# Moving a context prefix's load and normalization into the loop over the latent tokens

## The chip, the core and the metric

The kernel runs on one core of a Trainium2 chip. Five engines work side by side, each in its own fixed order: TensorE (PE, with its weight loads shown as PEld), VectorE (DVE), ScalarE (ACT), GpSimd (POOL) and SyncE (SP), whose queue issues the transfers here. They wait for each other through semaphores. Matrix products end in PSUM, eight banks of 512 columns; everything else lies in the on-chip memory SBUF. The metric is device microseconds of one execution; the times given are medians of several. Beside that time stands the span of a profiled execution, from its first to its last recorded instruction.

## What is computed

One layer of a hybrid diffusion backbone: 512 latent tokens x, 256 context tokens ctx, width 1024, all float32. The part that matters here is the beginning. Two modulation vectors come from the condition vectors, both token sets are normalized and modulated with them, and one wide projection is applied to both.

```python
mod   = silu(c) @ w_ada + b_ada            # for x
mod_c = silu(c_ctx) @ w_ada + b_ada        # for ctx
h  = rms_norm(x,   g_norm1) * (1.0 + sc1)  + sh1
hc = rms_norm(ctx, g_norm1) * (1.0 + csc1) + csh1
aq, ak, av, dq, dk, dv, dz, da, db, ga, gd = split_cols(h @ w_in)
caq, cak, cav, cdq, cdk, cdv, cdz, cda, cdb, cga, cgd = split_cols(hc @ w_in)
```

Here `da` and `db` give the decay and the write strength of a gated delta rule ("the gates"), `dk` its keys, which pass a short convolution and a silu. Windowed attention, the delta rule over chunks in both directions, the merge of the branches and the MLP follow; they are the other nine tenths of the time.

## The kernel before

Tokens lie along the columns and the 1024 features along eight groups of 128 partitions, so x is eight tiles of 128x512 and ctx eight of 128x256. For accuracy every float32 product is made as three: each operand is split into a high and a low part, and `mm3` (L308 to L315) adds high times high, high times low and low times high. A weight tile is 128 output columns with all eight feature groups; `wload` makes its high part on ACT (L259) and its low part on DVE (L262).

The start runs as follows. `rms` (L278 to L290) takes the mean square of x: ACT squares (L281), DVE adds (L284), PE sums over partitions with a matrix of ones (L286), ACT makes rstd with Ln and Exp (L148). Then a loop runs over the eight feature groups, `kt` from 0 to 7. In each turn:

- `modulate` (L317 to L321) makes h of this group for x: DVE scales (L318), ACT adds the shift and rounds to the high part (L319), DVE makes the low part (L320). ACT also keeps the unrounded h (L333) in a list `tx`.
- `ada` and `columns` make the modulation of the group two turns ahead: a 1 MB tile of w_ada is loaded (L206), multiplied on PE (L210), copied by ACT (L234), turned into columns on PE (L239) and finished on DVE (L242, L243).
- The early weight tiles, four tiles of `dk`, are loaded in turns 0 and 1, and each turn multiplies its h with all four of them, in four banks that stay open over the loop.

In turn 5 (`CTXAT` is 7, `AHEAD` is 2) the SP queue takes the weights of the gates, `wab`, and the context, two transfers, behind the last tile of w_ada.

After the loop `ab_strips` (L299 to L305) makes the gates of x: sixteen float32 products with 32 output rows each (L302), read from `tx`. A dependency that makes no wait, only an order for the scheduler, holds each group of four behind the h at position 3 of the list. Then come the statistics of the context (`rms` again), its modulation in eight steps (L318 to L320 with 256 columns, and L358 for the unrounded copy), and the context's strips. Next the four early weight tiles are multiplied with the context (96 matmuls of 256 columns), with the convolutions of `dk` on ACT and DVE (L611 to L613) among them. Then follow the gates' arithmetic (L665 to L677, exponentials and logarithms on ACT), four silus, sums of squares (L629), and the first tile of the next weights (`wh`, `wl`).

The order of the instructions on each engine is not exactly that of the program. A scheduler fixes it at compile time: it lets an engine take the earliest instruction of the program that its estimate of times says is ready. The waits are added by it as well, from the memory that instructions read and write.

Buffers come from a ring, `Arena`, of 167 units of 256 columns. `alloc` takes the next free units behind the last ones taken, and `free` releases them at once in the program's order; whoever gets the same units later waits on the chip for the earlier users. So which buffer falls on which units decides some of the waits. Banks of PSUM come from a second ring of eight.

Of the kernel before, what the change touches and what calls it, by code (L numbers as in the profile page):

```python
# [11 lines left out]
AF = mybir.ActivationFunctionType  # L12
# [10 lines left out]
LEAD = 0  # L23
ATT = 32
NHALF = 3
CTXAT = 7
WARM = 3, 6
NONES = 16
AHEAD = 2
# [9 lines left out]
KT = D // P  # L39
SEQ = 512  # L40
CTX = 256
# [58 lines left out]
def tile_layer(ctx: ExitStack, tc: tile.TileContext, I: dict, out: bass.AP, dbg=None):  # L100
    nc = tc.nc
    V, A, G, PE = nc.vector, nc.scalar, nc.gpsimd, nc.tensor
# [19 lines left out]
    alloc, bank = mem.get, lambda n=1: banks.get(n * 512)  # L122
# [14 lines left out]
    nosync = mybir.DependencyInfo(mybir.DependencyClass.NoSync, mybir.DependencyReason.DATA)  # L137
    actg = {"set": None, "head": None, "ops": []}

    def act(out_, in_, func, **kw):  # L140

        sets = TABLES.get(func)
        if sets and actg["set"] not in sets:
            head = A.preload_act_table_set(sets[0])
            for o in actg["ops"]:
                tc.add_manual_dep(head.ins, o.name, nosync, reason="table sets")
            actg.update(set=sets[0], head=head.ins, ops=[head.ins])
        r = A.activation(out_, in_, func, **kw)  # L148
        if sets:
            tc.add_manual_dep(r.ins, actg["head"].name, nosync, reason="table sets")  # L150
            actg["ops"].append(r.ins)
        return r
# [48 lines left out]
    def ada(kt):  # L201


        rp_ = banks.get(512, True)
        wb = alloc(2048)
        nc.sync.dma_start(out=wb.ap, in_=I["wada1"][kt])  # L206
        for half in range(2):
            for g in range(4):
                k = half * 4 + g
                PE.matmul(rp_[32 * g:32 * g + 32, :256], scond[:, k], wb[:, k * 256:(k + 1) * 256],  # L210
                          start=(half == 0), stop=(half == 1))
        wb.free()
        return rp_

    def warm(bank_, n):

        for _ in range(n):
            PE.matmul(bank_[:, 384:512], ones, ones, start=True, stop=True)

    xs_, cs_ = alloc(8 * SEQ), alloc(8 * CTX)  # L220
# [3 lines left out]
    modA = const.tile([P, KT, 2], F32, name="modA")  # L224
    modS = const.tile([P, KT, 2], F32, name="modS")
# [3 lines left out]
    def columns(kt, rp_):  # L229

        if kt == 0:
            warm(rp_, WARM[0])
        rb_ = alloc(256)
        row_[kt] = A.activation(rb_.ap, rp_[:, :256], AF.Copy)  # L234
        rp_.free()
        mp_ = banks.get(512, True)
        mp = mp_[:, 0:4].rearrange("p (h n) -> p h n", h=2)
        for half in range(2):
            PE.matmul(mp[:, half, :], rb_[:, half * P:(half + 1) * P], prm[:, 184:186], start=True, stop=True)  # L239
        rb_.free()  # L240

        V.tensor_scalar(modA[:, kt, :], mp[:, 0, :], bada1[:, kt:kt + 1], g1[:, kt:kt + 1], op0=ALU.add, op1=ALU.mult)  # L242
        V.tensor_scalar(modS[:, kt, :], mp[:, 1, :], bada[:, kt:kt + 1], None, op0=ALU.add)  # L243
        if kt == 0:
            warm(mp_, WARM[1])
        mp_.free()

    def wfetch(src, n=KT):
        raw = sb.tile([P, KT, P], F32, tag="wr", bufs=NWR, name=nm("wr"))[:, :n]
        nc.sync.dma_start(out=raw, in_=src)  # L250
        return raw

    def wload(src, n=KT, bufs=None, raw=None):
        raw = wfetch(src, n) if raw is None else raw
        if bufs:
            hi, lo = (b.ap.rearrange("p (k c) -> p k c", k=KT) for b in bufs)
        else:
            hi, lo = (sb.tile([P, KT, P], F32, tag=t, bufs=NWS, name=nm(t))[:, :n] for t in ("wh", "wl"))
        h = A.activation(r32(hi), raw, AF.Copy)  # L259
        if not early:  # L260
            tc.add_manual_dep(h.ins, row_[0].ins.name, nosync, reason="behind the first row")
        V.tensor_tensor(r32(lo), raw, hi, op=ALU.subtract)  # L262
        return r32(hi), r32(lo)

    early, EARLY = [], {T_DK: 0, T_DK + 1: 0, T_DK + 2: 0, T_DK + 3: 1}

    def load_early(raw=None):
        bb = ebufs[2 * len(early):][:2]
        early.append((wload(I["win"][list(EARLY)[len(early)]], bufs=bb, raw=raw), bank()))

    xt = [xs_[:, k * SEQ:(k + 1) * SEQ] for k in range(KT)]
    ct_ = [cs_[:, k * CTX:(k + 1) * CTX] for k in range(KT)]
    rstd = alloc(768)
    rx, rc = rstd[:, :512], rstd[:, 512:768]

    def rms(src, nt, n, r):

        ss = bank()  # L278
        for i in range(nt):
            b = alloc(1024)  # L280
            A.activation(b.ap, src[:, i * 1024:(i + 1) * 1024], AF.Square)  # L281
            w = 512
            while w >= n:
                V.tensor_tensor(b[:, :w], b[:, :w], b[:, w:2 * w], op=ALU.add)  # L284
                w //= 2
            PE.matmul(ss[:, :n], ones, b[:, :n], start=(i == 0), stop=(i == nt - 1))  # L286
            b.free()
        act(r, ss[:, :n], AF.Ln, bias=epsc, scale=1.0 / D)
        ss.free()
        act(r, r, AF.Exp, scale=-0.5)  # L290
# [6 lines left out]
    tx, tc_ = [], []  # L297

    def ab_strips(ab, hs, s):  # L299

        for g in range(4):
            m = PE.matmul(ab[32 * g:32 * g + 32], wab[:, 4 * s + g], hs[g][0].ap, start=(s == 0), stop=(s == 1))  # L302
            tc.add_manual_dep(m.ins, hs[3][1].ins.name, nosync, reason="strips together")
        for _ in range(4):
            hs.pop(0)[0].free()  # L305


    def mm3(acc, w, xs, start=True, stop=True, ks=None):  # L308
        ks = list(range(len(xs))) if ks is None else ks
        n = len(ks)  # L310
        for i, k in enumerate(ks):
            xhi, xlo = xs[i]
            PE.matmul(acc, w[0][:, k, :], xhi, start=(start and i == 0), stop=False)  # L313
            PE.matmul(acc, w[0][:, k, :], xlo, start=False, stop=False)  # L314
            PE.matmul(acc, w[1][:, k, :], xhi, start=False, stop=(stop and i == n - 1))  # L315

    def modulate(t, src, r, sc, sh, hi, lo, eng=V):  # L317
        V.scalar_tensor_tensor(t, src, sc, r, op0=ALU.mult, op1=ALU.mult)  # L318
        A.activation(r32(hi), t, AF.Identity, bias=sh)  # L319
        eng.scalar_tensor_tensor(r32(lo), t, sh, hi, op0=ALU.add, op1=ALU.subtract)  # L320
        return r32(hi), r32(lo)  # L321

    H, HCb = alloc(8 * 1024, True), alloc(8 * 512, True)
    hx, hc = [], []
    columns(1, ada(1))
    raw1 = wfetch(I["win"][T_DK + 1])
    for kt in range(KT):
        t = alloc(512)
        o = kt * 1024
        hx.append(modulate(t.ap, xt[kt], rx, modA[:, kt, 0:1], modS[:, kt, 0:1],  # L330
                           H[:, o:o + 512], H[:, o + 512:o + 1024]))
        h = alloc(512)
        tx.append((h, A.activation(h.ap, t.ap, AF.Identity, bias=modS[:, kt, 0:1])))  # L333
        t.free()
        if kt == 0:
            load_early(raw0)
            load_early(raw1)
        if kt + AHEAD < KT:
            columns(kt + AHEAD, ada(kt + AHEAD))
        if kt + AHEAD == CTXAT:  # L340
            nc.sync.dma_start(out=wab_.ap, in_=I["wab"])
            for k4 in range(KT // 4):
                nc.sync.dma_start(out=cs_[:, k4 * 1024:(k4 + 1) * 1024], in_=I["ctxT"][k4])
        if len(early) < len(EARLY):
            load_early()
        for (w, acc), k0 in zip(early, EARLY.values()):
            for k in range(kt + 1) if kt == k0 else (kt,):
                mm3(acc.ap, w, [hx[k]], start=(k == 0), stop=(k == KT - 1), ks=[k])
    abx = bank()
    for s in range(2):  # L350
        ab_strips(abx.ap, tx, s)
    rms(cs_, 2, CTX, rc)
    for kt in range(KT):
        t = alloc(256)
        o = kt * 512
        hc.append(modulate(t.ap, ct_[kt], rc, modA[:, kt, 1:2], modS[:, kt, 1:2],
                           HCb[:, o:o + 256], HCb[:, o + 256:o + 512]))
        tc_.append((t, A.activation(t.ap, t.ap, AF.Identity, bias=modS[:, kt, 1:2])))  # L358
    abc = bank()
    for s in range(2):  # L360
        ab_strips(abc[:, :CTX], tc_, s)
# [299 lines left out]
    t, t2 = alloc(TOK), alloc(TOK)  # L661
# [601 lines left out]
    for g in range(2):  # L1263
        cs_ = slice(g * 1024, g * 1024 + 1024)
        V.tensor_tensor(nv(on[:, cs_]), nv(ot_[:, cs_]), bc(osf[:, g * 16:g * 16 + 16], HD), op=ALU.mult)

    for qq in range(2):
# [3 lines left out]
        for a in range(2):  # L1271
            n = 2 * qq + a
            t = alloc(512)
# [259 lines left out]
```

## Time and profile before

| | us |
|---|---|
| runs shown | 942.98, 939.68, 942.67 |
| median | 942.67 |
| the profiled execution's own time | 939.99 |
| its span | 937.9 |

On the profile's page PE is busy 96% of the span, DVE 63%, ACT 48%. Its section on the chain that ended last follows the work back from the last instruction and says how much of the span each engine holds; that, and not the busy share, says what the end waits for. The timeline lists instructions in order of time, with the number merged into a row after "x", and in brackets the idle time of the engine before them and what ended it. The windows view gives, for a stretch of time, each engine's busy time, the clock that the throttle granted to PE (1.00 is full) and what the DMA engines moved. The transfers at the start, from their list up to 60 us: eight tiles of w_ada of 1024 KB with a median of 10.6 us from issue to landing, nine weight tiles of 512 KB with 8.1 us, two context transfers of 512 KB with 7.2 us, one of 128 KB for `wab` with 4.8 us.

### The profile page before, as it was taken

To read this page: it belongs to the slowest core of one execution; us is meant where nothing else is said; L and a number is where in the kernel's file an instruction comes from. 1 tells how busy PE (TensorE), PEld (TensorE's weight loads), DVE (VectorE), ACT (ScalarE), POOL (GpSimd) and SP (SyncE) were. 2 spreads that over 40 slices of the span, in tenths; PEclk is the share of its full clock that TensorE was granted. 3 is DMA by queue.
4 is the path that set the end of the run, shared out by engine and by line. 5 is a ranking of instruction groups with operands and counts; after the bars stand their busy time and mean duration, and the time that the engine had idled before them with its cause. 6 is when DMAs were issued, how large, how long until landed. Compare 5 with 4: busy or idle time off the path is not lost.

```text
span 937.9 us, 18101 instructions
## 1 busy us (share of the span) xinstructions
PE 900.3 (96%) x7706; PEld 724.5 (77%) x7706; DVE 595.2 (63%) x1017; ACT 451.6 (48%) x832; POOL 12.1 (1%) x26
## 2 busy tenths in 40 slices
PE   7979889999999999989999999999999999999998
PEld 4658567877777677778888888988888888888886
DVE  4485799997777899258865886982455235434411
ACT  5467845247667977575645424661243125213400
POOL 0000000000000001000000000000000000000000
PEclk9989999999999999999999999999999999999999
DMA  9631021210000132324523485481344124222111
GB/s 360 267 115 51 24 70 45 68 46 24 23 1 23 45 96 88 114 93 149 169 81 134 148 272 154 140 290 42 109 151 144 46 68 152 96 68 90 45 42 48
DMA packets 28448, 98.32 MB, mean 105 GB/s; under 512 B 3536, under 2 KB 4176, under 8 KB 27344
## 3 DMA queue, kind: packets, MB, share of 16 engines
q1 hardware_dynamic: 28368, 97.18, 31.5%
q8 instruction: 60, 0.98, 0.4%
q14 instruction: 20, 0.16, 0.1%
HBM read 95.07 MB, written 2.10 MB: 104 GB/s over the span
## 4 chain that ended last, share of the span: by engine, by line
PE 76%; DVE 12%; ACT 7%; DMA 3%; issue 2%; SPq 0%; DVEq 0%; ACTq 0%
PE banks L313 16%; PE banks L314 16%; PE banks L315 16%; PE banks L989 10%; PE banks L1034 2%; PE banks L1101 2%; DMA wa<-in_wada 2%; PE banks L564 1%; PE banks L1132 1%; PE banks L1113 1%; DVE wl L262 1%; ACT m L148 1%; PE banks L570 1%; DVE m L819 1%; DVE m L818 1%
## 5 line engine op out<-in xcount | busy, mean ns | idle before, releaser
L313 PE MATMUL banks<-m,m 128*128 128x512 f32 (+1 forms) x600 | 224.2, 379 | 5.1 <-ACT m L319 4.6
L314 PE MATMUL banks<-m,m 128*128 128x512 f32 (+1 forms) x600 | 225.2, 378 | 0.0
L315 PE MATMUL banks<-m,m 128*128 128x512 f32 (+1 forms) x600 | 225.2, 378 | 0.0
L259 ACT ACTIVATE m<-wr 128x1024 fp32r<-128x1024 f32 x68 | 71.9, 1059 | 157.9 <-PE banks L314 79.9
L313 PEld LDWEIGHTS banks<-m,m 128*128 128x128 f32 x600 | 112.8, 190 | 27.6 <-ACT m L319 6.6
L314 PEld LDWEIGHTS banks<-m,m 128*128 128x128 f32 x600 | 113.2, 190 | 22.4 <-issue 1.2
L315 PEld LDWEIGHTS banks<-m,m 128*128 128x128 f32 x600 | 113.1, 189 | 21.8 <-issue 1.6
L262 DVE TENSOR_TENSOR m<-wr,m 128x1024 fp32r<-128x1024 f32 x68 | 83.2, 1224 | 69.7 <-PE banks L314 34.2
L989 PE MATMUL banks<-m,wh 128*128 128x512 f32 x320 | 104.0, 399 | 0.0
L313 PE MATMUL banks<-m,wh 128*128 128x512 f32 (+1 forms) x280 | 102.8, 368 | 0.3 <-ACT wh L259 0.2
L315 PE MATMUL banks<-m,wl 128*128 128x512 f32 (+1 forms) x280 | 100.4, 361 | 1.5 <-DVE wl L262 1.4
L314 PE MATMUL banks<-m,wh 128*128 128x512 f32 (+1 forms) x280 | 101.6, 363 | 0.0
L1417 DVE SCALAR_TENSOR_TENSOR m<-banks,modT,m 128x512 f32<-128x512 f32 x32 | 24.0, 750 | 101.0 <-PE banks L315 101.0
L262 DVE TENSOR_TENSOR wl<-wr,wh 128x1024 fp32r<-128x1024 f32 (+1 forms) x58 | 62.3, 1073 | 25.8 <-ACT wh L259 25.6
L259 ACT ACTIVATE wh<-wr 128x1024 fp32r<-128x1024 f32 (+1 forms) x58 | 54.5, 940 | 30.0 <-PE banks L314 16.2
L989 PEld LDWEIGHTS banks<-m,wh 128*128 128x128 f32 x320 | 59.1, 188 | 12.2
L989 PE MATMUL banks<-m,wl 128*128 128x512 f32 x160 | 64.9, 406 | 0.0
L315 PEld LDWEIGHTS banks<-m,wl 128*128 128x128 f32 x280 | 53.3, 191 | 9.7 <-DVE wl L262 2.3
L313 PEld LDWEIGHTS banks<-m,wh 128*128 128x128 f32 x280 | 53.4, 191 | 8.8 <-ACT wh L259 0.7
L314 PEld LDWEIGHTS banks<-m,wh 128*128 128x128 f32 x280 | 53.5, 191 | 7.0 <-issue 0.4
L184 ACT ACTIVATE m<-m 128x512 fp32r<-128x512 f32 (+1 forms) x56 | 35.2, 631 | 48.2 <-DVE m L1400 20.8
L185 DVE TENSOR_TENSOR m<-m,m 128x512 fp32r<-128x512 f32 (+1 forms) x56 | 38.3, 689 | 18.8 <-ACT m L184 18.3
(236 smaller groups left out, 1290.0 us busy)
## 6 DMA issues: line engine op xcount, KB each, us to landing
wr<-in_wm SPq DMA_DIRECT2D x64, 512.0 KB, 3.5
wr<-in_win SPq DMA_DIRECT2D x38, 512.0 KB, 3.6
wa<-in_wada SPq DMA_DIRECT2D x32, 512.0 KB, 4.2
m<-in_wada SPq DMA_DIRECT2D x8, 1024.0 KB, 10.6
m<-in_xT SPq DMA_DIRECT2D x8, 512.0 KB, 5.2
wr<-in_wbr SPq DMA_DIRECT2D x16, 256.0 KB, 2.7
wr<-in_wout SPq DMA_DIRECT2D x8, 512.0 KB, 4.4
out<-m SPq DMA_DIRECT2D x8, 256.0 KB, 2.0
```

Source lines behind the costliest of these rows:

```text
L148: r = A.activation(out_, in_, func, **kw)
L184: A.activation(r32(hi), src, AF.Copy)
L185: (eng or V).tensor_tensor(r32(lo), src, hi, op=ALU.subtract)
L259: h = A.activation(r32(hi), raw, AF.Copy)
L262: V.tensor_tensor(r32(lo), raw, hi, op=ALU.subtract)
L313: PE.matmul(acc, w[0][:, k, :], xhi, start=(start and i == 0), stop=False)
L314: PE.matmul(acc, w[0][:, k, :], xlo, start=False, stop=False)
L315: PE.matmul(acc, w[1][:, k, :], xhi, start=False, stop=(stop and i == n - 1))
L989: PE.matmul(acc.ap, w[x][:, k, :], hx[k][y], start=(k == p == 0), stop=(k == KT - 1 and p == 2))
L1034: PE.matmul(pa.ap, w[x][:, j, :], r32(Q[y][:, :, j, :]), start=(j == p == 0), stop=(j == 3 and p == 2))
L1101: PE.matmul(z[r, x * 256 + q * HD:x * 256 + (q + 1) * HD], src[q][r, col(c):col(c) + CH], S[r, q * HD:(q + 1) * HD], start=True, stop=True)
L1417: V.scalar_tensor_tensor(xn_[ct], acc.ap, modT[:, 3, ct:ct + 1], xn_[ct], op0=ALU.mult, op1=ALU.add)
```

## The change

`CTXAT` goes from 7 to 3: the transfers of `wab` and of the context are put into turn 1 of the loop, and the load of the fourth early weight tile, in the same turn, is placed ahead of them. The statistics of the context are made at the end of turn 3 and its modulation at the ends of turns 4 to 7, two groups each. The order dependency of the strips goes to the last entry of the list: for the first four strips that is the eighth h, for the last four of the remaining list the same one. The computation is the same.

```diff
-CTXAT = 7
+CTXAT = 3
...
-            tc.add_manual_dep(m.ins, hs[3][1].ins.name, nosync, reason="strips together")
+            tc.add_manual_dep(m.ins, hs[-1][1].ins.name, nosync, reason="strips together")
...
+    def context(kt):
+
+        t = alloc(256)
+        o = kt * 512
+        hc.append(modulate(t.ap, ct_[kt], rc, modA[:, kt, 1:2], modS[:, kt, 1:2],
+                           HCb[:, o:o + 256], HCb[:, o + 256:o + 512]))
+        tc_.append((t, A.activation(t.ap, t.ap, AF.Identity, bias=modS[:, kt, 1:2])))
+
     columns(1, ada(1))
...
             columns(kt + AHEAD, ada(kt + AHEAD))
+        if len(early) < len(EARLY):
+            load_early()
         if kt + AHEAD == CTXAT:
             nc.sync.dma_start(out=wab_.ap, in_=I["wab"])
             for k4 in range(KT // 4):
                 nc.sync.dma_start(out=cs_[:, k4 * 1024:(k4 + 1) * 1024], in_=I["ctxT"][k4])
-        if len(early) < len(EARLY):
-            load_early()
         for (w, acc), k0 in zip(early, EARLY.values()):
             for k in range(kt + 1) if kt == k0 else (kt,):
                 mm3(acc.ap, w, [hx[k]], start=(k == 0), stop=(k == KT - 1), ks=[k])
+        if kt == 3:
+            rms(cs_, 2, CTX, rc)
+        if kt > 3:
+            context(2 * kt - 8)
+            context(2 * kt - 7)
     abx = bank()
     for s in range(2):
         ab_strips(abx.ap, tx, s)
-    rms(cs_, 2, CTX, rc)
-    for kt in range(KT):
-        t = alloc(256)
-        o = kt * 512
-        hc.append(modulate(t.ap, ct_[kt], rc, modA[:, kt, 1:2], modS[:, kt, 1:2],
-                           HCb[:, o:o + 256], HCb[:, o + 256:o + 512]))
-        tc_.append((t, A.activation(t.ap, t.ap, AF.Identity, bias=modS[:, kt, 1:2])))
     abc = bank()
```

## The prediction

> **What bounds the kernel now.** I read the page first: the busy times, then the chain that ended last.
>
> ```profile
> span 937.9 us, 18101 instructions
> PE 76%; DVE 12%; ACT 7%; DMA 3%; issue 2%; SPq 0%; DVEq 0%; ACTq 0%
> ```
>
> PE carries three quarters of the chain, so a change pays where PE stands still or runs slowly. The change touches only the first tenth of the span. So I cut the start into stretches: the loop over x (in two parts), the pause behind it, the context products (the 96 matmuls of 256 columns on the four early tiles), and the two stretches after. Columns: start and end, length, then busy time and count of PE, PEld, DVE, ACT and POOL, PEclk, DMA share, GB/s.
>
> ```profile
> 17.50:35.00 17.50, 14.73 (x98) 8.98 (x98) 9.81 (x17) 8.79 (x14) 0.00 (x0) 1.00 0.81 324
> 35.00:55.90 20.90, 20.90 (x143) 14.58 (x141) 9.29 (x20) 8.76 (x15) 0.73 (x1) 1.00 0.75 265
> 55.90:64.40 8.50, 3.41 (x22) 1.01 (x21) 8.47 (x16) 6.36 (x11) 0.00 (x0) 0.86 0.06 22
> 64.40:79.30 14.90, 14.90 (x111) 13.81 (x112) 12.27 (x27) 9.41 (x23) 0.73 (x1) 0.85 0.23 80
> 79.30:93.20 13.90, 13.40 (x113) 11.82 (x112) 5.80 (x14) 13.37 (x18) 0.00 (x0) 0.88 0.01 1
> 93.20:104.40 11.20, 9.07 (x68) 4.47 (x67) 4.93 (x8) 8.49 (x15) 0.00 (x0) 0.85 0.01 1
> ```
>
> From 35.0 to 55.9 PE is never idle, while DVE and ACT each use under half. From 55.9 to 64.4 it is the reverse: DVE is full and PE works 3.41 of 8.50 us. The timeline shows what PE does there; the bracket is idle time before the instruction and what ended it.
>
> ```profile
> 55.93 1.92 PE L302 MATMUL banks<-m,m 128*32 128x512 f32 x16
> 57.01 2.00 ACT L281 ACTIVATE m<-m 128x1024 f32<-128x1024 f32 x2 [0.29 <-PE banks L302]
> 59.93 0.67 PE L286 MATMUL banks<-m,ones 128*128 128x256 f32 x2 [2.08 <-DVE m L284]
> 61.53 0.79 PE L286 MATMUL banks<-m,ones 128*128 128x256 f32 x2 [0.93 <-DVE m L284]
> 64.40 1.22 PE L313 MATMUL banks<-m,m 128*128 128x256 f32 x4 [2.08 <-ACT m L319]
> 74.87 0.28 PE L313 MATMUL banks<-m,m 128*128 128x256 f32 x1
> 77.27 0.28 PE L313 MATMUL banks<-m,m 128*128 128x256 f32 x1
> 79.43 0.40 PE L313 MATMUL banks<-m,wh 128*128 128x512 f32 x1
> ```
>
> The context statistics begin only after the gate strips (L302): the square on ACT is released by them. The data were not late; the ring of buffers explains it. Walking its allocations in program order, the square's buffer falls on units that held an h of the loop, which the strips read. Then squares, adds on DVE among the convolutions, the sum on PE, the rstd and the first modulation run one after another: PE idles 2.08 + 0.93 + 2.08 = 5.09 us.
>
> The granted clock falls as well:
>
> ```profile
> 20.00:25.00 5.00, 3.75 (x27) 1.83 (x27) 2.86 (x5) 2.02 (x4) 0.00 (x0) 1.00 1.02 418
> 25.00:30.00 5.00, 3.75 (x26) 2.42 (x29) 2.86 (x5) 2.61 (x4) 0.00 (x0) 1.00 0.72 300
> 60.00:65.00 5.00, 1.99 (x7) 1.10 (x8) 4.97 (x11) 3.15 (x7) 0.00 (x0) 0.70 0.00 0
> 65.00:70.00 5.00, 5.00 (x32) 4.52 (x31) 4.97 (x13) 4.54 (x12) 0.00 (x0) 0.62 0.01 3
> ```
>
> It is 0.70 and 0.62 around the pause. At full clock a context product takes (77.27 - 74.87) / 20 = 0.12 us, the 20 matmuls between those starts being counted in the trace.
>
> **The change, part by part.**
>
> *The transfers.* The gate weights (128 KB) and two context transfers (512 KB each), 1.18 MB, move on SP's queue from behind the eighth modulation tile to behind the fourth early weight tile, ahead of four modulation tiles of 1 MB.
>
> ```profile
> 10.64 0.44 SPq L250 DMA_DIRECT2D wr<-in_win  x1
> 13.87 0.33 SPq L206 DMA_DIRECT2D m<-in_wada  x1
> 35.34 1.07 PE L210 MATMUL banks<-m,m 128*32 128x256 f32 x16
> 38.83 0.42 PE L210 MATMUL banks<-m,m 128*32 128x256 f32 x4
> ```
>
> At 13.87 SP had been waiting for a free buffer, so three more issues fit in front. At 418 GB/s the added bytes take 2.8 us. The queue is full until about 28.6 (0.72 of the slice 25 to 30), by when the sixth modulation tile has landed; it now lands near 31.4, and PE reads it at 38.83. The fifth lands one tile (2.5 us) earlier, near 28.9, and is read at 35.34. Slack is over 6 us on both: cost nothing. If the cover were gone, the 2.8 us would show. The two later tiles wait for buffers and are issued when the queue has drained. The context lands near 26, well before the fourth turn.
>
> *Statistics and modulation.* Nothing is added to the work; it moves forward. Its rows, all in 55.9 to 79.4 before:
>
> ```profile
> L358 ACT ACTIVATE m<-m,modS 128x256 f32<-128x256 f32 x8 | 3.5, 499 | 0.6 <-DVE m L320 0.6
> L319 ACT ACTIVATE m<-m,modS 128x256 fp32r<-128x256 f32 x8 | 3.5, 498 | 0.6 <-DVE m L318 0.6
> L318 DVE SCALAR_TENSOR_TENSOR m<-m,modA,m 128x256 f32<-128x256 f32 x8 | 3.4, 467 | 0.0
> L320 DVE SCALAR_TENSOR_TENSOR m<-m,modS,m 128x256 fp32r<-128x256 f32 x8 | 3.4, 467 | 0.0
> L281 ACT ACTIVATE m<-m 128x1024 f32<-128x1024 f32 x2 | 2.0, 1048 | 0.3 <-PE banks L302 0.3
> L284 DVE TENSOR_TENSOR m<-m 128x512 f32<-128x512 f32 x2 | 1.4, 688 | 0.0
> L284 DVE TENSOR_TENSOR m<-m 128x256 f32<-128x256 f32 x2 | 0.8, 415 | 0.0
> L148 ACT ACTIVATE m<-banks,epsc 128x256 f32<-128x256 f32 x1 | 0.5, 473 | 1.3 <-PE banks L286 1.3
> L148 ACT ACTIVATE m<-m 128x256 f32<-128x256 f32 x1 | 0.4, 416 | 0.0
> ```
>
> DVE: 3.4 + 3.4 + 1.4 + 0.8 = 9.0 us. ACT: 3.5 + 3.5 + 2.0 + 0.5 + 0.4 = 9.9 us. In the PE-bound part of the loop DVE would then hold 9.29 + 9.0 = 18.3 of 20.9 us and ACT 8.76 + 9.9 = 18.7. Both fit, barely, and the statistics can begin before 35, where both have gaps too. By the same walk along the ring their buffers now fall on units of the third modulation tile, read long before, so the wait on the strips is gone. What can go wrong is order: each of the last turns has a short chain, PE's modulation product, ACT's copy, PE's sum, DVE's columns, and a context operation of 0.4 us ahead of a link delays it, and with it whatever PE has queued behind. PE's four sum matmuls (L286) also enter the full loop: 0.67 + 0.79 us by their rows, less the overlap of their ends, 1.2 us. For disturbed order I bound below by 0 (PE has earlier turns' matmuls to run meanwhile) and above by 4.5 us (in each of the last four turns a link on ACT waits for a pair of context operations, 2 x 3.5 / 8 = 0.9 us, and once for a square, 1.0); I take 1.0, near the lower end, because half of both engines is empty there.
>
> *The strips held together.* The first four strips now wait for the eighth h instead of the fourth. Queued behind them on PE are the context strips and products. Before, all sixteen already ran in one piece at 55.93, after the last product of x, whose turn needs that turn's values as well: 0 us either way. The context strips, before in two pieces, become one.
>
> *Sum, first step: the start of the next weight tile* (79.43, the first product with wh). After: the loop's end 55.9, + 1.2 sums, + 1.0 order, + 1.9 strips of x, + 1.3 context strips (half as many columns, bounded by the 1.9), + 96 x 0.12 = 11.5 products = 72.8. Gain 6.6 us: 5.1 of idle, the rest mostly the clock, which has no pause left to fall in.
>
> The convolutions (DVE) and their banks don't become late: without 9.0 us of context work DVE has 8.47 + 12.27 - 9.0 = 11.7 us left for the 17 us from 55.9 to 72.8.
>
> *Second step: what is late next.* From 78.41 ACT runs the gates, table loads and silus without a pause, and PE waits for what follows.
>
> ```profile
> 78.41 0.85 ACT L148 ACTIVATE m<-m 32x768 f32<-32x768 f32 x1 [0.18 <-DVE m L667]
> 85.63 3.04 ACT L148 ACTIVATE m<-m 128x768 f32<-128x768 f32 x4
> ```
>
> ACT is busy 13.37 of 13.90 us from 79.3 to 93.2. PE idles 0.50 and 2.13 us in the last two stretches, and at clocks of 0.88 and 0.85 loses up to 0.12 x 13.9 + 0.15 x 11.2 = 3.3 us. The gates need only the strips and adds on DVE, so they can run beside the products: from some 66, 12 us earlier, against 6.6 for PE. Silus need the last product, near 73, and then run without the 6 us of gates ahead. So ACT gains more than PE and PE's waits shrink. Bounds: 0 (the gates keep their place behind) to 2.6 + 3.3 = 5.9 us. I take 2.9, about half: of the idle time 2, of the clock 0.9, since the small matmuls that precede its dip remain.
>
> Total 6.6 + 2.9 = 9.5 us. From there the kernel is the same on every engine and should shift as a whole.
>
> The sum is against the profiled execution, 939.99 us (span 937.9 and 2.1 around it): 930.5. That is 2.7 below the median shown, 942.67. I forecast medians: 942.7 - 9.5 = **933.2**.
>
> **The rivals.**
>
> *A, given back.* The pause closes but the loop is disturbed by 4.5 us, not 1.0, and the ACT stretch gives nothing: 6.6 - 3.5 = 3.1 us, 939.6. For it: 18.7 of 20.9 us on ACT leaves little room. Against: the gaps before 35.
>
> *B, not moved.* ACT takes the statistics late after all, behind the strips, because their order or a buffer holds them: about 0, 942.7. Against: the ring.
>
> *C, slower: the turn's chain becomes the bound.* If ACT's and DVE's context work (9.9 + 9.0 us) ran ahead of the links rather than beside them, the loop would grow by up to 18.9 us; it turns slower beyond 9.5. At three quarters, 14.2, it gives 942.7 + 4.7 = 947.4. Against: the two engines work at the same time, and PE has a turn of products in stock.
>
> *D, clock.* The pause is spread as many small waits over turns 4 to 7, and the clock falls there: at half clock the stretch 38.83 to 55.93 would lose up to 17.1 us, 942.7 - 9.5 + 17.1 = 950.3. Against: from 20 to 30 PE was idle a quarter of the time in small waits, and the clock stayed at 1.00. [...]
>
> **How the numbers follow.** Forecast 0.67; A 0.17; B 0.06; C 0.07; D 0.03. The forecast's terms run from 6.6 - 3.5 + 0 to 7.6 + 5.9, that is 3.1 to 13.5 us: 929.2 to 939.6. The runs shown lie 3.3 us apart, so I widen to **928 to 940**; B, C and D are left out. 0.5%, about what a measurement of this kernel can tell from no change, is 4.7 us: faster below 938.0. Of the forecast's chance 0.03 lies above that, where few of its terms come true; of A's, 0.06 lies below. Faster 0.64 + 0.06 of A = 0.70; same 0.03 + 0.11 + 0.06 + 0.01 of C = 0.21; slower 0.09.
>
> **What would show it.** Right: squares (L281, second pair) before 40 us; context modulation (L318, 256 columns) between 36 and 54; PE without idle from 35 to about 73; a granted clock of 1.00 from 55 to 72; the first product with wh near 73; the first silu near 74, not 85.63. Wrong: an x product or modulation product in turns 4 to 7 that waits for ACT or DVE by more than 1 us in sum; strips that start after 59; a gain at the wh product that is gone by 130 us, which would mean that another engine, DVE first, bounds what follows.

## The result and the profile after

The changed kernel takes 934.46 us (median of 7 runs, 928.64 to 935.11), the kernel before 942.49 in the same measurement: a ratio of 0.991, 95% interval 0.9884 to 0.9937. Measured once more, on another chip (e9 below), it was 933.89 against 939.09, 0.9935 (0.9911 to 0.9958). So 5 to 8 us were gained where 9.5 had been forecast. The profiled execution took 934.46 us, against 939.99 before, 5.5 less.

The page of the changed kernel: its span, and the chain that ended last.

```profile
span 932.4 us, 18104 instructions
PE 71%; DVE 12%; ACT 9%; DMA 5%; issue 3%; SPq 0%; DVEq 0%; ACTq 0%
```

The windows view of the changed kernel over the same stretches as before (columns as there).

```profile
17.50:35.00 17.50, 15.00 (x88) 8.50 (x88) 7.34 (x15) 7.04 (x11) 0.00 (x0) 0.80 0.87 342
35.00:55.90 20.90, 19.65 (x136) 13.12 (x135) 15.45 (x35) 15.30 (x29) 0.73 (x1) 1.00 0.62 222
55.90:64.40 8.50, 8.50 (x53) 5.09 (x54) 6.35 (x11) 6.00 (x12) 0.00 (x0) 1.00 0.32 101
64.40:79.30 14.90, 14.90 (x121) 14.11 (x113) 11.82 (x22) 6.84 (x14) 0.73 (x1) 1.00 0.22 75
79.30:93.20 13.90, 13.10 (x103) 10.61 (x102) 4.82 (x12) 12.69 (x19) 0.00 (x0) 0.88 0.00 0
93.20:104.40 11.20, 9.07 (x96) 4.92 (x98) 8.23 (x12) 9.29 (x18) 0.00 (x0) 0.85 0.01 1
```

The pause is gone: from 55.9 to 64.4 PE is busy all of 8.50 us (3.41 before), and the clock stays at 1.00 to 79.3. Three other things are new. The clock is 0.80 in the first stretch, where it was 1.00. PE has 1.25 us of idle time in the loop, where it had none. And the last two stretches are as slow as before: ACT at 12.69 of 13.90, clocks of 0.88 and 0.85.

The timeline of the changed kernel, PE and ACT, at the places that the prediction named:

```profile
36.53 2.00 ACT L281 ACTIVATE m<-m 128x1024 f32<-128x1024 f32 x2
41.02 1.07 PE L210 MATMUL banks<-m,m 128*32 128x256 f32 x16
58.16 1.04 PE L302 MATMUL banks<-m,m 128*32 128x512 f32 x2
62.09 2.78 PE L302 MATMUL banks<-m,m 128*32 128x512 f32 x30
64.80 0.39 PE L313 MATMUL banks<-m,m 128*128 128x256 f32 x1
76.05 0.40 PE L313 MATMUL banks<-m,wh 128*128 128x512 f32 x1
```

The squares start at 36.53 with no wait for the strips. The modulation product of group 4, at 35.34 before, comes at 41.02. The loop ends near 62, not 55.9; behind it the strips, all but one of x and of the context together, take 2.8 us in one piece and the products 11.2 us. The first product with wh comes at 76.05 instead of 79.43: **3.4 us gained, where 6.6 had been forecast.** The gain stays between 2.5 and 3.4 us up to 200 us, is 4.4 us at 305 us and 5.5 us at the end of the span. What adds the last microsecond, near 550 us, was not looked into.

The next view explains a part. These are windows of the kernel before (first fence) and of the changed kernel (second), laid on the places where the granted clock is low.

```profile
62.00:68.80 6.80, 4.71 (x21) 4.40 (x21) 6.77 (x17) 5.85 (x15) 0.00 (x0) 0.50 0.01 2
89.30:92.70 3.40, 3.40 (x14) 3.01 (x14) 1.66 (x5) 3.06 (x6) 0.00 (x0) 0.50 0.00 0
215.60:219.00 3.40, 3.40 (x51) 2.42 (x50) 2.46 (x5) 2.26 (x4) 0.00 (x0) 0.51 0.36 123
```

```profile
21.80:25.20 3.40, 3.28 (x20) 1.59 (x20) 1.11 (x2) 0.68 (x2) 0.00 (x0) 0.53 1.00 393
28.60:32.00 3.40, 3.09 (x13) 1.90 (x17) 1.30 (x2) 0.88 (x2) 0.00 (x0) 0.54 0.84 349
86.70:90.10 3.40, 3.40 (x16) 3.11 (x16) 1.76 (x6) 3.37 (x6) 0.00 (x0) 0.53 0.00 0
```

Taken in slices of 0.2 us, the clock in these two profiles is 1.00 or 0.50, apart from the slices in which it changes: ten falls to 0.50, one of 6.8 us (62 to 68.8 of the kernel before), nine of 3.4. The changed kernel lost the long fall in the pause, and the one at 216 us, but this profile of it has two falls in the loop that the profile of before doesn't have. By the products of groups 2 and 3 (L210, at 23.88 and 31.35 against 23.81 and 29.46, after a start that was 0.4 earlier) they cost 2.3 us up to there.

### The profile page after: what moved, and what is told of

Its sections match the earlier page's. It is cut to its first block, busy times and chain, and to the rows that moved or that the text cites. A ratio compares the mean times of both kernels' runs of the same rounds, so it can differ in the third digit from the quotient of the medians.

```text
span 932.4 us, 18104 instructions
## 1 busy us (share of the span) xinstructions
PE 900.4 (97%) x7706; PEld 723.8 (78%) x7706; DVE 595.8 (64%) x1017; ACT 451.4 (48%) x832; POOL 12.1 (1%) x26
## 4 chain that ended last, share of the span: by engine, by line
PE 71%; DVE 12%; ACT 9%; DMA 5%; issue 3%; SPq 0%; DVEq 0%; ACTq 0%
PE banks L313 15%; PE banks L314 15%; PE banks L315 15%; PE banks L996 8%; DMA wr<-in_wm 2%; PE banks L1041 2%; DMA wa<-in_wada 2%; ACT m L148 2%; PE banks L1108 2%; DVE wl L262 1%; PE banks L1139 1%; PE banks L571 1%; PE banks L1120 1%; DVE m L185 1%; DVE m L826 1%
## 5 line engine op out<-in xcount | busy, mean ns | idle before, releaser
L185 DVE TENSOR_TENSOR m<-m,m 128x512 fp32r<-128x512 f32 (+1 forms) x56 | 38.3, 689 | 18.8 <-ACT m L184 18.3
```

The lines of the kernel that those rows point to most:

```text
L185: (eng or V).tensor_tensor(r32(lo), src, hi, op=ALU.subtract)
```

## The experiments

All times are medians, each beside runs of the kernel before on the same chip; ratios are against those and, as they stand on record, need not be the quotient of the two medians. "Mean clock" is the mean over a kernel's runs of the clock granted over its span.

**e1, the transfers alone.** The kernel before, with `CTXAT` 3 and the early tile's load ahead of them:

```diff
-CTXAT = 7
+CTXAT = 3
+        if len(early) < len(EARLY):
+            load_early()
         if kt + AHEAD == CTXAT:
...
-        if len(early) < len(EARLY):
-            load_early()
```

> Only the transfers move (behind the fourth early weight tile); statistics, modulation and strips stay as before. Theory: placing the context ahead of four modulation tiles makes the scheduler put PE's modulation product of group 4 behind the stored x products, so turn 4 begins some 5 us late, while the statistics still wait for the strips: first product with wh at 80 to 83 us, time 943 to 946. Rival, the transfers cost nothing and the loop lost its time to the added work alone: modulation product of group 4 near 35, first product with wh at 79.4, time as before, 942.5.

942.1 us, ratio 1.0016 (0.9999 to 1.0032). The timeline of e1:

```profile
41.54 1.07 PE L210 MATMUL banks<-m,m 128*32 128x256 f32 x16
43.20 1.04 PE L302 MATMUL banks<-m,m 128*32 128x512 f32 x2
44.71 1.05 PE L302 MATMUL banks<-m,m 128*32 128x512 f32 x4
```

The mechanism was right: group 4's modulation product moves to 41.54 although only transfers were moved in the program, and single strips scatter into the loop. A strip is listed as two instructions, so the sixteen rows of L302 for x are eight products of the program; one alone takes 1.04 us, all eight together 1.92. The first product with wh comes at 84.92, but in the slowest of the twelve runs (945.65 us), whose mean clock is 0.986 (0.9896 over the twelve). What the moved transfers cost is not settled: 1.3 us by the medians, anything from 0 to 3 us by the interval. That the scheduler believed the modulation tile to be late is argued only; that the transfers' place moves the product is shown, here and in e2.

**e2, the transfers two turns later.** The changed kernel with

```diff
-CTXAT = 3
+CTXAT = 5
```

> The changed kernel with the transfers two turns later, behind the sixth modulation tile (CTXAT 5 in place of 3). Theory: the modulation product of group 4 comes back to 35 to 36 us from 41, the loop over x ends 2 to 4 us earlier than at 62, and the kernel gains 1.5 to 3 us on the changed one: 931.5 to 933 by the median. Rival, PE's work in the loop is only reordered and its sum bounds it: loop end and time as the changed kernel, 934.5.

933.39 us, ratio 0.9929 (0.9905 to 0.9953): not to be told from the changed kernel's 0.991 and 0.9935. The product is back in its place and PE's loop still ends at 60.6, with 18 of the 96 context products already done; 2.3 of the 62 us in the changed kernel were the clock. So the rival holds: the loop's work was only in another order. But the profiled execution of e2 (930.31 us, the fastest of its runs) had a clock of 1.00 throughout, and shows the new order without that disturbance. Its timeline and windows:

```profile
35.43 1.07 PE L210 MATMUL banks<-m,m 128*32 128x256 f32 x16
72.80 0.40 PE L313 MATMUL banks<-m,wh 128*128 128x512 f32 x1
```

```profile
20.00:25.00 5.00, 3.75 (x27) 1.84 (x27) 2.86 (x5) 2.04 (x3) 0.00 (x0) 1.00 1.02 415
25.00:30.00 5.00, 3.75 (x24) 2.41 (x28) 2.86 (x5) 2.67 (x4) 0.00 (x0) 1.00 1.02 414
```

The first product with wh is at 72.80, 6.6 us before the old place.

**e3, the strips' order as before.** The changed kernel with

```diff
-            tc.add_manual_dep(m.ins, hs[-1][1].ins.name, nosync, reason="strips together")
+            tc.add_manual_dep(m.ins, hs[3][1].ins.name, nosync, reason="strips together")
```

> The changed kernel with the strips' order as before (behind the h at position 3). Theory: the scheduler scatters single strips among the x products and each lone strip holds the whole array for about 1 us where four together take 0.4: with some five pieces 2 to 3 us more, 936 to 938. Rival, the strips only fill time in which PE waits in turns 4 and 5: same as the changed kernel, 934.5.

934.49 us, ratio 0.9931 (0.991 to 0.9952). Some strips do scatter (from 36.90 on), and it costs nothing that can be measured: the rival. The theory also counted four strips together at 0.4 us, which no run shows: here a row of eight instructions, so four strips, takes 1.06 us (at 64.41), as long as one strip alone (1.05, at 36.90). The forecast of 0 us for this edit holds.

**e4, the gates first.** The changed kernel with the block that makes the gates (from `nega` to the end of `t2.free()`, L662 to L686 of the changed kernel) moved ahead of the line `kT = [...]`, so ahead of the context products:

```diff
+    nega = const.tile([32, 1], F32, name="nega")
+    act(nega, alog[0:32], AF.Exp)
...
     kT = [alloc(TOK, True) for _ in range(4)]
     for q, (w, acc) in enumerate(early):
...
-    nega = const.tile([32, 1], F32, name="nega")
-    act(nega, alog[0:32], AF.Exp)
```

> The changed kernel with the gates' arithmetic ahead of the context products and convolutions in the program. Theory: the gates came late because their adds on DVE stand behind the convolutions; moved ahead, ACT's gate chain begins before 70 instead of 75.9, the first silu comes at 77 to 79 instead of 83.1, and 2 to 4 us are gained: 930.5 to 932.5. Rival, DVE is full there and the convolutions become late in turn, so that products wait for their banks: 934 to 936.

936.17 us, ratio 0.9948 (0.993 to 0.9966), at a mean clock of 0.991 (0.993 for e3, on the same chip). The chain of the gates does move: the table load ahead of the silus is at 75.80, 81.84 in the changed kernel. But PE waits for a late convolution, as the rival said:

```profile
69.85 0.35 PE L313 MATMUL banks<-m,m 128*128 128x256 f32 x1 [1.86 <-DVE m L620]
```

Behind this wait the clock falls (0.62 from 71.4 to 74.8), and PE takes sums of squares before the next weight tile, whose first product is at 84.41, 76.05 in the changed kernel. In this form, no gain.

**e5, buffers of their own.** The kernel before, with two buffers for the squares:

```diff
+    own = [alloc(1024), alloc(1024)]
...
-            b = alloc(1024)
+            b = own[i] if own else alloc(1024)
...
-    rms(cs_, 2, CTX, rc)
+    rms(cs_, 2, CTX, rc, own)
```

> The kernel before with two buffers of its own for the squares of the context, so that they no longer fall on the ring's units that the strips read; nothing else moves. Theory: the squares and adds run in ACT's and DVE's free time before 56, PE's pause of 5.1 us of idle shrinks to the last links (rstd, first modulation, about 3 us), and the time falls by 2 to 4 us. Rival, the squares wait for something else (the data, the order): pause and time as before.

941.54 us, ratio 1.0014 (0.9991 to 1.0037). Squares and adds do run before 56 now, so the ring did hold them. But in PE's order the sums stand behind the strips, and the wait remains. Its timeline:

```profile
57.20 1.92 PE L303 MATMUL banks<-m,m 128*32 128x512 f32 x16
59.06 1.13 PE L286 MATMUL banks<-m,ones 128*128 128x256 f32 x4
63.74 0.58 PE L314 MATMUL banks<-m,m 128*128 128x256 f32 x1 [3.55 <-ACT m L320]
```

PE idles 3.55 us instead of 5.09, close to the 3 us foretold, but no gain in time can be measured. Taking away a wait for memory wasn't enough; the work had to be earlier in the program.

**e6, the pause filled.** The kernel before, with 22 products of ones by ones that nobody reads, for PE to run in the pause:

```diff
     rms(cs_, 2, CTX, rc)
+    fb_ = bank()
+    for _ in range(22):
+        PE.matmul(fb_[:, :P], ones, ones, start=True, stop=True)
+    fb_.free()
```

> The kernel before with 22 idle matmuls (ones times ones, into a free bank) behind the statistics in the program, for PE to run while it waits between the strips and the first context product. The waiting itself stays. Theory: half of the change's gain is the clock, which falls in that pause in every run: with the pause filled the half-clock window at 62 to 68.8 us is gone, the first product with wh comes at 77 to 78 instead of 79.4, and the time falls by 1.5 to 3 us. Rival, the clock falls for other reasons or the filling delays the sums: 0 or slower by 1 us.

937.61 us, ratio 0.9978 (0.9957 to 0.9999); the mean clock rises from 0.9892 for the runs beside it to 0.9956. The windows of e6:

```profile
55.90:64.40 8.50, 7.96 (x65) 6.17 (x64) 8.40 (x16) 6.21 (x10) 0.00 (x0) 1.00 0.04 13
64.40:79.30 14.90, 14.71 (x119) 13.27 (x120) 12.46 (x27) 10.89 (x25) 0.73 (x1) 1.00 0.23 80
```

The long fall of the clock is gone with the idling, and 2 us with it (0.1 to 4 by the interval), though the first context product begins no earlier: 64.59, 64.40 before. So the pause cost twice: its 5.09 us of idle time, and a clock of 0.50 from 62.0 to 68.8, where e6 has 1.00.

**e7 and e8, the loop filled.** The changed kernel and the kernel before, each with 20 such products in turns 1 to 4:

```diff
         if kt == 0:
             warm(mp_, WARM[1])
+        elif kt in FILLT:
+            warm(mp_, FILLN)
```

with `FILLT, FILLN = (1, 2, 3, 4), 5`.

> The changed kernel with five idle matmuls behind the columns in turns 1 to 4, 20 in all, 5 us of PE, in places where PE waits in short stretches. Theory: the clock that falls to half in some runs between 20 and 35 us does so because PE is idle a quarter of that time; with the waits filled those windows go, the runs lie closer together, mean clock 0.996 and more, median 930 to 932.5 against 934.5. Rival, the windows have nothing to do with these waits: same clock, 5 us more work, 935 to 938.

> The kernel before with the same 20 idle matmuls in turns 1 to 4. Theory: its early windows go too, but the one in the pause behind the loop stays: 1.5 to 3 us under before, 938.5 to 941, all runs within 2 us, mean clock 0.990 to 0.991. Rival as for the changed kernel with filling: 943 to 946.

e7: 933.09 us, ratio 0.9925 (0.9895 to 0.9955), mean clock 0.9953. e8: 937.47 us, 0.9978 (0.996 to 0.9996), 0.9937. In the kernel before the filling gains 2 us, within the 1.5 to 3 expected. Its profiled execution has a mean clock of 0.992; which of the falls are gone, this mean doesn't show. Over the runs its clock is higher than the 0.990 to 0.991 expected, and its runs lie 4.7 us apart, not 2. In the changed kernel time, clock and spread (928.88 to 936.09) all miss what was expected. The time can't be told from that without filling, and its profiled execution still has a mean clock of 0.992: inconclusive for the changed kernel alone.

**e9, the changed kernel again.**

> The changed kernel once more, for its spread and a second profile. Theory: its runs differ by how many half-clock windows of 3.4 us fall into the first 110 us; time rises by some 6.5 us for each 0.01 that the mean clock falls, from about 930 at 1.00; in a profile without early windows the loop over x ends near 59.5 instead of 62 us. Rival, the spread is something else: times that don't follow the clock.

933.89 us, mean clock 0.9938, and the profile has one early fall, not two (0.72 from 20 to 25 us, 0.94 from 25 to 30, 1.00 from 30 to 35); the first product with wh is at 74.87. Over its 13 runs here and in the first measurement, and 72 of the kernel before beside the experiments, time follows clock: a fit with one slope for both gives 7.3 us for each 0.01 of clock, and at equal clock 2.8 us (standard error 0.4) between the two kernels. The mean clocks are 0.9889 and 0.9944, worth 4.0 us. This is a fit over runs from several chips, not an experiment. The runs of before never reach a clock above 0.995.

**e10, e11, e12, combined.** e10: e2 with the filling of e7. e11: e10 with the gates first, as in e4. e12: the kernel before with the fillings of e6 and e8.

> The changed kernel with the transfers behind the sixth modulation tile and the 20 idle matmuls in turns 1 to 4. Theory: full clock in nearly all runs and turn 4 in its old place: 930 to 932. Rival, the place of turn 4 is worth nothing and only the filling counts: as the changed kernel with filling, 933.

> The same, and the gates' arithmetic ahead of the context products in the program. Theory: with the clock held, the earlier gate chain shows: first silu by 75 to 78 us, 928.5 to 930.5. Rival, it is paid back by PE waiting for late convolutions and silus: 931 to 934.

> The kernel before with both fillings: 20 idle matmuls in turns 1 to 4 and 22 in the pause. Its order of work stays that of before. Theory: what remains between it and the changed kernel with filling (933.1) is the schedule alone, 2 to 4 us: 935 to 937, mean clock 0.995 and more. Rival, the change is only a matter of the clock: 933.

e10: 933.75 us, ratio 0.994 (0.9917 to 0.9962); the rival, nothing gained, neither by the place of turn 4 nor by the filling (e9, on the same chip, has 933.89 without either). Its mean clock is 0.994, not the full clock expected. e12: 938.35, 0.9991 (0.9976 to 1.0006), at a mean clock of 0.9978. Neither theory's number: the clock is held, but the 42 products seem to cost as much as that brings; the first product with wh comes at 80.67, later than the 79.43 of before. What it does show is that the clock is not all of the change: on the same chip the old order with its 42 products takes 938 us at 0.998, and the new order 934 us at 0.994, both with 20 such products (e10) and without (e9). How much of these 4.5 us is the cost of the 42 products wasn't measured.

e11: **927.83 us**, ratio 0.9874 (0.985 to 0.9898), five runs from 926.62 to 929.08, mean clock 0.9988: faster than both kernels, and 0.6% faster than the changed one beside it (e9). Timeline and windows of e11 (its line 149 is 148 of the other kernels), and below them the first of the two windows in e10:

```profile
76.08 3.04 ACT L149 ACTIVATE m<-m 128x768 f32<-128x768 f32 x4
```

```profile
79.30:93.20 13.90, 13.90 (x111) 10.07 (x110) 6.77 (x13) 11.67 (x19) 0.00 (x0) 1.00 0.01 1
93.20:104.40 11.20, 9.95 (x246) 7.68 (x241) 8.72 (x15) 10.04 (x21) 0.00 (x0) 1.00 0.16 50
```

```profile
79.30:93.20 13.90, 12.67 (x94) 10.72 (x93) 4.83 (x12) 11.61 (x17) 0.00 (x0) 0.75 0.00 1
```

The silus come at 76.08 (83.13 in the changed kernel), PE no longer waits from 79.3 to 93.2, and the clock stays up there. e10 and e11 differ in the gates' place alone: 5.9 us, in the stretch where the prediction had put its second step and where the change by itself brings nothing. How much of it is order and how much clock wasn't taken apart; by the slope of the fit the two mean clocks would be worth some 3 us, an estimate. Nor does the gates' place gain this everywhere: the same edit on the changed kernel, e4, gained nothing, and there the first product with wh came at 84.41, here at 74.22, ahead of the silus. Why the scheduler made the two orders differ stays open.

## Why the prediction was right, and where it was off

**The transfers: cost nothing.** Not refuted in their time (e1 costs 0 to 3 us), wrong in what they touch: I counted issues, bytes and landings, and overlooked that the order of PE is fixed at compile time and changes with the transfers' place. Group 4's product moved by 5.7 us. e2 puts it back and gains nothing measurable, so in the changed kernel the miss was free.

**The strips' wait and the ring.** The squares start at 36.53, as foretold "before 40". The ring did cause the wait, but e5 shows that it wasn't the only thing that held the statistics back: PE's order would have.

**The loop, + 1.2 and + 1.0 us.** About right in size, though the loop ends later than foretold. In e2, at full clock, it ends 4.7 us later than before, 60.6 against 55.9, where 2.2 had been forecast. But 18 of the 96 context products and one strip are already done by then. From 55.93 to the first product with wh at 72.80 are 16.9 us; 3.7 of them are strips (0.98 and 2.71, from start to next start) and 11.5 the 96 products, which leaves 1.7 for sums and disturbed order. In the changed kernel the same reckoning, from group 3's product on (31.35, 29.46 before), leaves 3.0; 0.4 of that is the end of the second fall of the clock. That the strips start after 59, at 62.09, was named as a sign of being wrong; it came without the gain being lost. DVE and ACT were busy 15.45 and 15.30 us of 20.9, not 18.3 and 18.7: the last context work came after 55.9, in a loop that ran to 62.

**First step, 6.6 us.** Met in an execution at full clock: 72.80 in e2, whose transfers lie two turns later, against a forecast of 72.8. That it is met to the tenth is luck: the strips took 0.5 us more than forecast, sums and disturbed order 0.5 less. In the profiled execution of the changed kernel it was 3.4 us. Of the difference 2.3 are the two falls of the clock in the loop; the rest is about the size of PE's idle time there, 1.25 us. An execution of the changed kernel at full clock was not profiled.

**The clock.** Here the prediction failed. It took "the clock, which has no pause left to fall in" for granted and gave case D 0.03 because "from 20 to 30 PE was idle a quarter of the time in small waits, and the clock stayed at 1.00". The same stretches in the changed kernel:

```profile
20.00:25.00 5.00, 3.82 (x18) 1.89 (x22) 2.87 (x5) 1.55 (x3) 0.00 (x0) 0.70 1.01 403
25.00:30.00 5.00, 3.75 (x20) 2.28 (x13) 2.86 (x5) 2.67 (x4) 0.00 (x0) 0.84 1.04 426
```

PE is busy for the same 3.75 to 3.8 of 5.00 us, and the clock is 0.70 and 0.84; in e2, with 3.75 again, 1.00. One execution with a full clock proved nothing: with the same waits it is low in one run and full in the next. Nor does it take the change: in e5, whose order on PE up to 35 us is that of the kernel before, the clock falls in the same place.

```profile
22.40:25.80 3.40, 3.33 (x20) 1.74 (x20) 1.06 (x2) 0.64 (x2) 0.00 (x0) 0.51 1.02 417
```

All ten falls in the profiles of the two kernels go to 0.50, nine for 3.4 us and one for 6.8, and in the loop their places differ from run to run: two in the changed kernel, one in e9, none in e2. What sets them off there was not shown. It was not case D's place, though: the changed kernel's falls, near 22 and 29 us, lie in turns 1 and 2, whose work on PE the change left as it was, and not in the turns to which the context work was added.

**Second step, 2.9 us.** This failed: it took the gates as free to run from 66 us. "The gates need only the strips and adds on DVE, so they can run beside the products: from some 66." The changed kernel's timeline, DVE and ACT:

```profile
70.32 0.68 DVE L674 TENSOR_TENSOR m<-m,banks 32x512 f32<-32x512 f32 x1
75.42 0.42 DVE L674 TENSOR_TENSOR m<-m,banks 32x256 f32<-32x256 f32 x1
75.93 0.85 ACT L148 ACTIVATE m<-m 32x768 f32<-32x768 f32 x1 [2.08 <-DVE m L674]
83.13 3.05 ACT L148 ACTIVATE m<-m 128x768 f32<-128x768 f32 x4
```

The strips were done at 65, but the six adds stand behind the convolutions in DVE's order, from 70.32 to 75.84, and ACT waits for them. So the chain moved by 2.5 us, less than PE's 3.4, and the sums of squares by 3.2: nothing of the second step came. I counted what the adds need and not what is queued ahead of them. e4 and e11 show that moving them moves the chain.

**The sum.** At equal clock the new order is worth 2.8 us by the fit; two profiles with a clock near full, e6 with the old order and its 22 added products (span 933.3, mean clock 0.999) and e2 with the new (928.5, 1.0), differ by 4.8. The clock adds some 4 in the mean, by the fit. So the measured 5 to 8 us are first-step idle time and clock, less what the loop gave back. No engine behind 104 us took anything back, as forecast, and the range of 928 to 940 holds the result. That the median came so near to 933.2 is in part luck: the second step's 2.9 us didn't come, and the clock, counted at about 1.5 us in the first step and 0.9 in the second, brought more than that.

## What to carry over

The pause of PE had two prices here, 5.09 us of idle time and a clock of 0.50 from 62.0 to 68.8; filling it with throwaway products (e6) showed how much the second was, 2 us. Before a moved block is credited with starting early, look at what stands ahead of its first instruction on each engine, and at what a moved transfer does to the order that the compiler fixes. And where runs of one kernel differ by some tenths of a per cent, put each run's time beside its mean clock before the schedules are compared.

## What was not expected of the hardware

Three things. Executions of one kernel on one chip differ by over 1%, and that along the clock: the 30 runs of the kernel before beside e5 to e8 lie between 935.51 us (clock 0.994) and 946.92 us (0.984). The clock fell in the pause (0.50 from 62.0 to 68.8) although PE was never idle there for more than 2.08 us at a time; it worked 3.41 of 8.50 us, and 1.14 of the 3.40 us from 58.6 to 62.0, just ahead of the fall. And a high clock isn't worth any price: e12 had 0.998 in the mean, nearly the best of all, and was as slow as the kernel before.
